# Splitting the queries into high and low parts where they are projected, and loading a layer's small constants earlier

## The chip, the cores and the metric

The kernel runs on one core of one Trainium2 chip. The metric is the device time of one execution in microseconds (us): the median of the runs. The engines are TensorE (PE, with its weight loads PEld), VectorE (DVE), ScalarE (ACT), GpSimd (POOL) and SyncE (SP), which only issues DMAs here. Each takes its own instructions in order.

## What is computed

Two layers of an encoder over a sequence of 2048 positions and 1024 features, in float32. Each layer normalises its input, projects it, sends the parts of the projection through three groups of heads, multiplies each by a gate, and projects back:

```python
for layer in range(2):
    h = rms_norm(x, norm_pre[layer])
    proj = h @ w_in[layer]                      # 1024 -> 4128
    (gq, gk, gv, gg, gaf, gab, dq, dk, dv, dg, hq, hzf, hzb, hi, hg) = split(proj)
    y_a = gla_branch(gq, gk, gv, gg, gaf, gab, wa2_f, ba_f, wa2_b, ba_b, ...)   # gated linear attention
    y_b = diff_branch(dq, dk, dv, dg, lq1, lk1, lq2, lk2, ...)                  # softmax attention
    y_c = hgrn_branch(hq, hzf, hzb, hi, hg, lb, ...)                            # gated recurrence
    x = x + rms_norm(concat(y_a, y_b, y_c) @ w_out[layer], norm_post[layer])
```

The change touches `diff_branch`. It has 4 heads with two softmaxes each, so 8 query and 8 key heads of 64 features. Queries and keys are turned by rotary positions (`x1 cos - x2 sin`, `x2 cos + x1 sin`, on two halves of 32 features), scores are taken, and `w = softmax(s0) - lam * softmax(s1)` weighs the values. `lam` comes from four vectors of 64 numbers per layer. `gla_branch` needs a small matrix of 16 x 128 and a bias of 128 for each direction; these and `lam` are the layer's small constants.

## The kernel before

Matmuls take float32 operands that are split into a rounded high part and the low rest, and add three products (high x high, high x low, low x high). A layer runs in these stages.

**Projection, part 0 and part 1.** The list `first + rest` names 18 blocks of output columns. Part 0 runs all of them for the first 1024 positions, part 1 for the others. A block's weights are loaded by GpSimd's queue in two halves (`wraw`, 512 KB each, one buffer), cast to the high part `whi` on DVE, and the low part `wlo` is made on GpSimd (part 0) or DVE (part 1). Blocks 9 and 10 give the values, 11 and 12 the keys, 13 and 14 the queries (`do_qk`), 15 to 17 the gates (`do_gate`). `do_qk` works on two groups of 512 positions in a part: it loads the rotary table `cs` (512 KB, one buffer), makes two tiles of 512 columns on TensorE (24 matmuls each, line 297), and for each half turns them with two products on DVE (lines 335, 337) and a sum on GpSimd (line 338). A key half is then rounded on ScalarE (line 343), its rest is taken on GpSimd (line 344), and both are stored to `dr_k` in DRAM. A query half is stored once, unsplit, to `dr_q` (line 340). The tiles `u`, `z` and `rh` share one tag of 7 buffers with those of the gates. TensorE writes to 8 banks of PSUM in part 0 and to 4 in part 1. In part 1 the chunked scans of the two other groups of heads are run in between, in steps given by the list `SCHED`; their memory is given back after block 14.

**Attention.** 64 units (4 heads x 16 blocks of 128 queries), in an order written out by hand for TensorE, ScalarE, DVE and GpSimd. For every two units `load_q` fetches 256 queries of both softmaxes: four DMAs of 64 KB, since the rows of each half are wanted twice (the keys' high and low parts lie in 128 partitions), a cast to the high part on GpSimd (line 730) and a subtraction for the low part (line 732). Scores are two matmuls each, `qh` and `ql` against the same keys (lines 875, 876). GpSimd also runs the recurrence of the states (lines 775, 778) at the start of this stage.

**Output projection.** 16 tiles of 128 positions (line 1045); in layer 0 it also opens layer 1's first weights and normalised inputs.

The small constants are loaded in `layer_constants`, after block 0 of part 0: 12 DMAs on SP and some ten short operations, in layer 1 as in layer 0. Block 1 (`do_gate(512, ...)`) yields the low-rank columns `low`, which block 2 transposes (line 414).

The rest of the order is made by a planner ahead of time, from its own estimate of when each operand is ready. SP issues its DMAs in the planned order, and an issue that waits holds up those behind it.

Of the kernel before, what the change touches and what calls it, by code (L numbers as in the profile page):

```python
# [11 lines left out]
F32 = mybir.dt.float32  # L12
F32R = mybir.dt.float32r
BF16 = mybir.dt.bfloat16
U8 = mybir.dt.uint8
AF = mybir.ActivationFunctionType
ALU = mybir.AluOpType
AX = mybir.AxisListType
# [3 lines left out]
P = 128  # L22
L = 2048
# [37 lines left out]
def tile_hybrid_encoder(  # L61
# [9 lines left out]
    nc = tc.nc  # L71

    const = ctx.enter_context(tc.tile_pool(name="const", bufs=1))
    lay = ctx.enter_context(tc.tile_pool(name="lay", bufs=1))
    dram = ctx.enter_context(tc.tile_pool(name="dram", bufs=1, space=DRAM))
# [23 lines left out]
    dr_qh = dram.tile([2, P, L], F32, name="dr_qh")  # L99
    dr_fh = dram.tile([2, 2, P, L], F32, name="dr_fh")  # L100
    dr_kh = dram.tile([2, 2, P, L], F32, name="dr_kh")
    dr_q = dram.tile([8, 2, 32, L], F32, name="dr_q")
    dr_k = dram.tile([8, 2, 2, 32, L], F32, name="dr_k")
    dr_v = dram.tile([L, 512], F32, name="dr_v")
    dr_vs = dram.tile([L, 512], F32, name="dr_vs")
# [17 lines left out]
    def one_bank(shape, name, key="m"):  # L123
        return psum[key][1].tile(shape, F32, tag="one", name=name, bufs=2 if key == "t" else 4)
# [102 lines left out]
    def open_w(l):  # L227
# [9 lines left out]
            nc.gpsimd.tensor_tensor(lo[:, ks], raw, hi[:, ks].bitcast(F32), op=ALU.subtract)  # L237
        return st, (hi, lo)

    for l in range(DEPTH):  # L240
        lam_init = 0.8 - 0.6 * math.exp(-0.3 * l)
        xsrc = x[0] if l == 0 else dr_x
# [1 line left out]

        tst = lay.tile([P, 8, 16], F32, tag="tst", name="tst")
        tots = [lay.tile([P, 2, 16], F32, tag=f"tot_{ti}", name=f"tot_{ti}") for ti in range(3)]
        ls = lay.tile([P, 2], F32, tag="ls", name="ls")
        neglam = lay.tile([P, 1], F32, tag="neglam", name="neglam")
        wa2 = lay.tile([96, 2, P], F32R, tag="wa2", name="wa2")
        ba = lay.tile([P, 2], F32, tag="ba", name="ba")  # L250


        if l == 0:
# [2 lines left out]
        with ExitStack() as s1:  # L256
            ev = s1.enter_context(tc.tile_pool(name=f"ev{l}", bufs=EVB, side="right"))
# [6 lines left out]
            def acc(shape, name, part):  # L264
                turn[0] += 1
                return one_bank(shape, name, "m" if part == 0 and turn[0] % 2 else "s")

            def layer_constants():
                lv = ev.tile([P, 512], F32, tag="t", name="lv").rearrange("p (a n) -> p a n", n=64)
                lp = ev.tile([P, 512], F32, tag="t", name="lp").rearrange("p (a n) -> p a n", n=64)[:, :2]  # L270
                for i, a in enumerate((diff_lq1, diff_lk1, diff_lq2, diff_lk2)):
                    nc.sync.dma_start(lv[:, i], a[l:l + 1].to_broadcast([P, 64]))
                for i in range(2):
                    nc.vector.tensor_tensor(lp[:, i], lv[:, 2 * i], lv[:, 2 * i + 1], op=ALU.mult)
                nc.vector.reduce_sum(ls, lp, axis=AX.X)
                nc.scalar.activation(ls, ls, AF.Exp)
                nc.vector.tensor_tensor(neglam, ls[:, 1:2], ls[:, 0:1], op=ALU.subtract)
                nc.vector.tensor_scalar(neglam, neglam, -lam_init, None, op0=ALU.add)

                wraw = ev.tile([96, 512], F32, tag="t", name="wa").rearrange("p (d n) -> p d n", d=4)[:, :2]  # L280
                nc.vector.memset(wraw, 0.0)
                for d, (wa, b) in enumerate(((gla_wa2_fwd, gla_ba_fwd), (gla_wa2_bwd, gla_ba_bwd))):
                    for i in range(3):
                        nc.sync.dma_start(wraw[32 * i + 16 * d:32 * i + 16 * d + 16, d], wa[l])
                    nc.sync.dma_start(ba[:, d:d + 1], b[l].unsqueeze(1))
                nc.vector.tensor_copy(wa2, wraw)
                nc.vector.tensor_tensor(wa2[64:96], wraw[64:96], wa2[64:96].bitcast(F32), op=ALU.subtract)

            def wload(c0, n, part, halves=False):
                return wload_into(wp, l, nc.gpsimd if part == 0 else nc.vector, c0, n, halves)  # L290
# [33 lines left out]
            def do_qk(c0, cb, which, part):  # L324
                hc = slice(4 * cb, 4 * cb + 4)
                w = wload(c0 + 256 * cb, 256, part, halves=True)
                for g in (2 * part, 2 * part + 1):
                    sl = slice(g * 512, (g + 1) * 512)
                    cs = ev.tile([P, 2, 512], F32, tag="cs", name="cs", bufs=1)
                    nc.sync.dma_start(cs, c_rope[0 if which == "q" else 1, :, :, sl])  # L330
                    p1 = mm_ch(w, 0, g)
                    p2 = mm_ch(w, P, g)
                    for half, (a, b, op) in enumerate(((p1, p2, ALU.subtract), (p2, p1, ALU.add))):
                        u = ev.tile([P, 512], F32, tag="t", name="ru")
                        nc.vector.tensor_tensor(u, a, cs[:, 0], op=ALU.mult)  # L335
                        z = ev.tile([P, 512], F32, tag="t", name="rz")
                        nc.vector.tensor_tensor(z, b, cs[:, 1], op=ALU.mult)
                        nc.gpsimd.tensor_tensor(u, u, z, op=op)
                        if which == "q":
                            nc.sync.dma_start(dr_q[hc, half, :, sl], u)  # L340
                        else:
                            rh = ev.tile([P, 512], F32R, tag="t", name="rh")
                            nc.scalar.copy(rh, u)
                            nc.gpsimd.tensor_tensor(u, u, rh.bitcast(F32), op=ALU.subtract)
                            nc.sync.dma_start(dr_k[hc, half, 0, :, sl], rh.bitcast(F32))
                            nc.sync.dma_start(dr_k[hc, half, 1, :, sl], u)

# [132 lines left out]
            for i, b in enumerate(first + rest):  # L480
                b(0)
                if i == 0:
                    w_st.close()
                    xp_st.close()
                    hp = w_in_st.enter_context(tc.tile_pool(name=f"hp{l}", bufs=1, side="right"))
                    hhi += [hp.tile([P, 4, KC, P], F32R, name=f"hhi{g}") for g in (2, 3)]
                    hlo += [hp.tile([P, 4, KC, P], F32R, name=f"hlo{g}") for g in (2, 3)]
                    if l == 0:
                        load_constants()
                    layer_constants()  # L490
                if N0 < i <= N0 + 8:
                    prenorm_split(xn, (i - N0 - 1) % 4, hhi[2 + (i - N0 - 1) // 4], hlo[2 + (i - N0 - 1) // 4])
                if N0 <= i < N0 + 8:
                    xn = prenorm_load(npre, 8 + i - N0, ev, xsrc)
# [226 lines left out]
                kv[h] = (ks, v)  # L721

            def load_q(h, qp):
                qr = ak.tile([P, 2, 256], F32, tag="aq", name="aq", bufs=2)
                for half in range(2):
                    for s in range(2):
                        p0 = 64 * half + 32 * s
                        nc.sync.dma_start(qr[p0:p0 + 32], dr_q[2 * h:2 * h + 2, half, :, qp * 256:(qp + 1) * 256].rearrange("c p t -> p c t"))
                qh = ak.tile([P, 2, 256], F32R, tag="aqh", name="aqh", bufs=2)
                nc.gpsimd.tensor_copy(qh, qr)  # L730
                ql = ak.tile([P, 2, 256], F32R, tag="aql", name="aql", bufs=2)
                nc.gpsimd.tensor_tensor(ql, qr, qh.bitcast(F32), op=ALU.subtract)  # L732
                ga = ak.tile([P, 2, P], F32, tag="aga", name="aga", bufs=3)
                nc.sync.dma_start(
                    ga, dr_gate[qp * 256:(qp + 1) * 256, 256 + h * P:384 + h * P].rearrange("(j p) n -> p j n", p=P))
                qs_of[h, qp] = qh, ql, ga

            emitted = [0]
            for i, b in enumerate(first + rest):
                b(1)  # L740
                scans(LAG * SCHED[i] if i < SC_END else len(work))
                if i == SC_END:
# [4 lines left out]
                    ak = at_st.enter_context(tc.tile_pool(name=f"ak{l}", bufs=1, side="left"))  # L747
# [7 lines left out]
        with ExitStack() as s2:  # L755
# [14 lines left out]
            for i in range(14):  # L770
                for d in range(2):
                    c, sh = (i + 1, 1) if d == 0 else (14 - i, -1)
# [188 lines left out]
            with tc.manual_schedule(engines={getattr(mybir.EngineType, e) for e in ENGINES}):  # L961
                for f in range(4 * NU + 13):
# [51 lines left out]
                    if fw == 4 * KC + 8:  # L1014
                        wr_st.close()
                        op = s2.enter_context(tc.tile_pool(name=f"op{l}", bufs=2, side="right"))
# [51 lines left out]
            if l + 1 < DEPTH:  # L1068
                h_st, hhi, hlo, npre = open_h(l + 1)
                nc.sync.dma_start(npre, norm_pre[l + 1:l + 2].to_broadcast([P, D]))  # L1070
                w_st, w_first = open_w(l + 1)
                ep = s2.enter_context(tc.tile_pool(name=f"ep{l}", bufs=EPB, side="left"))
            for t in range(NT):
                y1, y2 = y2, out_prep(t + 1) if t + 1 < NT else None
                o = out_tile(t, *y1)
                if l + 1 < DEPTH:
                    if 1 <= t <= 8:
                        g, i = divmod(t - 1, 4)
                        prenorm_split(xn, i, hhi[g], hlo[g])
                    if t < 8:  # L1080
                        xn = next_scale(o)
# [53 lines left out]
```

## Time and profile before

| | |
|---|---|
| median of 3 runs | 3637.28 us (3628.71 to 3641.9) |
| profiled execution | 3641.44 us, span 3639.6 us |
| mean granted TensorE clock | 0.982 |
| TensorE busy | 3513.4 us (97%) |
| DVE, ScalarE, GpSimd busy | 2560.3, 1927.8, 1459.6 us (70%, 53%, 40%) |
| DMA | 430.49 MB, 118 GB/s over the span |

The span goes from the first to the last instruction; the execution's own time is 1.8 us longer. A matmul's end is modelled, so a busy TensorE need not be at its peak.

### The profile page before, as it was taken

The page shows a single profiled execution, that of the slowest core. Times are in us where ns is not written, and L with a number is a line of the kernel's source. Part 1 is how long each engine was busy: PE and PEld are TensorE (multiplying, and loading weights), DVE is VectorE, ACT ScalarE, POOL GpSimd, SP SyncE. Part 2 cuts the span into 40 slices and gives each one's busy share as a digit, 9 for nine tenths or more (in the row PEclk, how much of TensorE's full clock was granted, in tenths as well). Part 3 has the DMA queues.
Part 4 walks back from the last instruction along what each step waited for, and adds up shares of the span by engine and source line. Part 5 has one row for each costly group of instructions (what it writes and reads, how often), then busy time and mean ns, then how long its engine had stood idle before and what let it go on. Part 6 is the DMA issues. An engine that isn't in the chain of part 4 may idle for free.

```text
span 3639.6 us, 62254 instructions
## 1 busy us (share of the span) xinstructions
PE 3513.4 (97%) x23296; PEld 3159.5 (87%) x23296; DVE 2560.3 (70%) x4426; ACT 1927.8 (53%) x4340; POOL 1459.6 (40%) x1454
## 2 busy tenths in 40 slices
PE   8999999998989999999989999999999899999999
PEld 7898988987978999888878989889878799999887
DVE  5422699987389999985324227999863899999733
ACT  4520455542377888874225215555423778888722
POOL 4545410012476667720035454100125867767100
PEclk9999999998999999999999999999989999999999
DMA  4444544544441333213334444445444413322143
GB/s 155 127 139 134 151 128 139 157 126 139 136 133 34 120 109 97 73 43 132 120 109 128 140 136 139 140 145 154 133 123 141 125 42 120 118 83 73 34 139 116
DMA packets 293645, 430.49 MB, mean 118 GB/s; under 512 B 42400, under 2 KB 185312, under 8 KB 291040
## 3 DMA queue, kind: packets, MB, share of 16 engines
q1 hardware_dynamic: 268896, 333.71, 29.7%
q0 software_dynamic: 22336, 90.71, 8.4%
q8 instruction: 184, 3.01, 0.3%
q10 hardware_dynamic: 2112, 2.10, 0.2%
q14 instruction: 117, 0.96, 0.1%
HBM read 275.82 MB, written 152.57 MB: 118 GB/s over the span
## 4 chain that ended last, share of the span: by engine, by line
PE 67%; DVE 13%; DMA 10%; POOL 4%; issue 3%; ACT 1%; SPq 1%; DVEq 0%; POOLq 0%; ACTq 0%
PE pp L306 14%; PE pp L297 12%; PE pob L1045 10%; PE po L938 9%; PE s L875 5%; PE s L876 5%; PE pt L927 5%; DMA wraw<-in_w_in_dram 3%; DVE mx L880 3%; DMA cs<-c_rope 2%; PE pm L587 2%; DVE e L921 2%; PE pm L568 1%; DMA ust<-dr_u 1%; PE poi L825 1%
## 5 line engine op out<-in xcount | busy, mean ns | idle before, releaser
L880 DVE TENSOR_REDUCE mx<-s 128x1 f32<-128x1024 f32 x512 | 623.1, 1217 | 54.3 <-PE s L876 52.9
L889 ACT ACTIVATE e<-s,mx 128x1024 f32<-128x1024 f32 x512 | 571.7, 1121 | 74.8 <-DVE mx L880 53.3
L306 PE MATMUL pp<-wlo,hhi 128*128 128x256 f32 (+1 forms) x2048 | 589.1, 288 | 7.1 <-POOL wlo L224 6.8
L306 PE MATMUL pp<-whi,hhi 128*128 128x256 f32 (+1 forms) x2048 | 585.2, 286 | 5.5 <-DVE ru L335 4.5
L306 PE MATMUL pp<-whi,hlo 128*128 128x256 f32 (+1 forms) x2048 | 588.4, 287 | 0.5 <-DVE hlo L195 0.5
L938 PEld LDWEIGHTS po<-vt,wt 128*128 128x128 f32 x4096 | 537.6, 192 | 47.9 <-ACT o L945 5.8
L938 PE MATMUL po<-vt,wt 128*128 128x128 f32 x4096 | 544.0, 276 | 1.6 <-ACT o L945 1.6
L875 PE MATMUL s<-ks,aqh 128*128 128x512 f32 x1024 | 452.4, 442 | 19.8 <-ACT e L889 15.1
L214 POOL DMA_DIRECT2D wraw<-in_w_in_dram x124 | 96.0, 774 | 920.4 <-DVE wlo L224 348.6
L876 PE MATMUL s<-ks,aql 128*128 128x512 f32 x1024 | 407.2, 398 | 14.2 <-POOL aql L732 14.1
L297 PE MATMUL pp<-hhi,whi 128*128 128x512 f32 x1024 | 412.5, 403 | 0.0
L297 PE MATMUL pp<-hlo,whi 128*128 128x512 f32 x1024 | 411.2, 402 | 0.0
L297 PE MATMUL pp<-hhi,wlo 128*128 128x512 f32 x1024 | 409.0, 399 | 0.0
L306 PEld LDWEIGHTS pp<-wlo,hhi 128*128 128x128 f32 x2048 | 390.0, 190 | 10.5 <-POOL wlo L224 7.6
L306 PEld LDWEIGHTS pp<-whi,hhi 128*128 128x128 f32 x2048 | 391.9, 191 | 8.0 <-issue 4.8
L921 DVE SCALAR_TENSOR_TENSOR e<-e,gam 128x1024 f32<-128x1024 f32 x256 | 392.3, 1533 | 0.0
L306 PEld LDWEIGHTS pp<-whi,hlo 128*128 128x128 f32 x2048 | 390.5, 191 | 1.8 <-DVE hlo L195 0.7
L931 ACT COPY wt<-pt 128x512 f32<-128x512 f32 x512 | 301.3, 589 | 118.9 <-PE pt L927 115.7
L927 PE MATMUL pt<-ident,e 128*128 128x128 f32 x2048 | 310.1, 274 | 1.2 <-ACT wt L931 0.6
L927 PEld LDWEIGHTS pt<-ident,e 128*128 128x128 f32 x2048 | 241.9, 142 | 2.9 <-ACT wt L931 1.2
L875 PEld LDWEIGHTS s<-ks,aqh 128*128 128x128 f32 x1024 | 196.4, 192 | 51.7 <-ACT e L889 23.3
L297 PEld LDWEIGHTS pp<-hhi,whi 128*128 128x128 f32 x1024 | 194.6, 190 | 45.0 <-issue 0.9
(190 smaller groups left out, 7042.9 us busy)
## 6 DMA issues: line engine op xcount, KB each, us to landing
wraw<-in_w_in_dram POOLq DMA_DIRECT2D x116, 512.0 KB, 4.8
cs<-c_rope SPq DMA_DIRECT2D x32, 512.0 KB
dr_gate<-z SPq DMA_DIRECT2D x64, 256.0 KB
aq<-dr_q SPq DMA_DIRECT2D x256, 64.0 KB
ks<-dr_k POOLq DMA_DIRECT2D x16, 1024.0 KB, 8.0
y<-dr_y SPq DMA_DIRECT2D x32, 512.0 KB
dr_qs<-qt SPq DMA_DIRECT2D x48, 256.0 KB
qs<-dr_qs SPq DMA_DIRECT2D x24, 512.0 KB
```

What stands on the lines that cost most here:

```text
L214: nc.gpsimd.dma_start(raw[:, :, :n], w_in[l].rearrange("(k p) c -> p k c", p=P)[:, ks, c0:c0 + n])
L297: nc.tensor.matmul(ps.rearrange("p (a t) -> p a t", t=P), w[a][:, k, c:c + P], b[g][:, :, k], start=n == 0, stop=n == 3 * KC - 1)
L306: nc.tensor.matmul(ps, b[g][:, t % 4, k], w[a][:, k, :n], start=cnt == 0, stop=cnt == 3 * KC - 1)
L875: nc.tensor.matmul(s[:, i], self.qh[:, c, js], kk, start=True, stop=False)
L876: nc.tensor.matmul(s[:, i], self.ql[:, c, js], kk, start=False, stop=True)
L880: nc.vector.tensor_reduce(mx[:, k:k + 1], self.s[k].rearrange("p a n -> p (a n)"), axis=AX.X, op=ALU.max, negate=True)
L889: nc.scalar.activation(self.es[c][:, n * 1024:(n + 1) * 1024], self.s[kk].rearrange("p a n -> p (a n)"), AF.Exp, bias=self.mx[:, m:m + 1], ...
L921: nc.vector.scalar_tensor_tensor(es[0][:, hs], es[1][:, hs], gm[:, 8 + n:9 + n], es[0][:, hs], op0=ALU.mult, op1=ALU.add)
L927: nc.tensor.transpose(pt[:, i], self.es[0][:, (4 * q + i) * P:(4 * q + i + 1) * P], ident)
L931: nc.scalar.copy(wt, self.pt[q])
L938: nc.tensor.matmul(self.po, self.wt[q][:, i], self.v[:, k], start=k == 0, stop=k == NT - 1)
L1045: nc.tensor.matmul(pos[:, n], a[:, k], b[k][:, n * 512:(n + 1) * 512], start=cnt == 0, stop=cnt == 3 * KC - 1)
```

## The change

Queries are split as keys are: a half is rounded on ScalarE, its rest taken on GpSimd, and both parts are stored, each twice, to a `dr_q` that is laid out as the attention wants it. `load_q` becomes two plain loads of 256 KB, with no work on GpSimd. `layer_constants` and the tiles that it fills are moved out of the layer's stage; layer 0 calls it where it did, and for layer 1 it is called in layer 0's output projection, with the tiles of that stage's pool `ep`.

```diff
-    dr_q = dram.tile([8, 2, 32, L], F32, name="dr_q")
+    dr_q = dram.tile([8, 2, 2, 2, 32, L], F32, name="dr_q")
...
+    def layer_tiles():
+        neglam = lay.tile([P, 1], F32, tag="neglam", name="neglam")
+        wa2 = lay.tile([96, 2, P], F32R, tag="wa2", name="wa2")
+        ba = lay.tile([P, 2], F32, tag="ba", name="ba")
+        return neglam, wa2, ba
+
+    def layer_constants(l, pool, neglam, wa2, ba):
+        ls = lay.tile([P, 2], F32, tag="ls", name="ls")
...
+        if l == 0:
+            neglam, wa2, ba = consts = layer_tiles()
+        else:
+            neglam, wa2, ba = consts
...
+                        rh = ev.tile([P, 512], F32R, tag="t", name="rh")
+                        nc.scalar.copy(rh, u)
+                        nc.gpsimd.tensor_tensor(u, u, rh.bitcast(F32), op=ALU.subtract)
                         if which == "q":
-                            nc.sync.dma_start(dr_q[hc, half, :, sl], u)
+                            for dup in range(2):
+                                nc.sync.dma_start(dr_q[hc, 0, half, dup, :, sl], rh.bitcast(F32))
+                                nc.sync.dma_start(dr_q[hc, 1, half, dup, :, sl], u)
                         else:
-                            rh = ev.tile([P, 512], F32R, tag="t", name="rh")
-                            nc.scalar.copy(rh, u)
-                            nc.gpsimd.tensor_tensor(u, u, rh.bitcast(F32), op=ALU.subtract)
                             nc.sync.dma_start(dr_k[hc, half, 0, :, sl], rh.bitcast(F32))
                             nc.sync.dma_start(dr_k[hc, half, 1, :, sl], u)
...
                     if l == 0:
                         load_constants()
-                    layer_constants()
+                        layer_constants(0, ev, *consts)
...
             def load_q(h, qp):
-                qr = ak.tile([P, 2, 256], F32, tag="aq", name="aq", bufs=2)
-                for half in range(2):
-                    for s in range(2):
-                        p0 = 64 * half + 32 * s
-                        nc.sync.dma_start(qr[p0:p0 + 32], dr_q[2 * h:2 * h + 2, half, :, qp * 256:(qp + 1) * 256].rearrange("c p t -> p c t"))
                 qh = ak.tile([P, 2, 256], F32R, tag="aqh", name="aqh", bufs=2)
-                nc.gpsimd.tensor_copy(qh, qr)
                 ql = ak.tile([P, 2, 256], F32R, tag="aql", name="aql", bufs=2)
-                nc.gpsimd.tensor_tensor(ql, qr, qh.bitcast(F32), op=ALU.subtract)
+                for i, q in enumerate((qh, ql)):
+                    nc.sync.dma_start(q.bitcast(F32), dr_q[2 * h:2 * h + 2, i, :, :, :, qp * 256:(qp + 1) * 256]
+                                      .rearrange("c a d p t -> (a d p) c t"))
...
                 ep = s2.enter_context(tc.tile_pool(name=f"ep{l}", bufs=EPB, side="left"))
+                consts = layer_tiles()
+                layer_constants(l + 1, ep, *consts)
```

## Rows read from the trace of the kernel before

**Rows 1.** The page's first line.

```profile
span 3639.6 us, 62254 instructions
```

**Rows 2.** Waits of PE: line <- releaser: us in total, times, longest us.

```profile
PE s L876 <- POOL aql L732: 14.1, 4, 4.3
...
PE ppa L414 <- ACT low L390: 11.4, 3, 5.1
...
PE s L875 <- POOL aqh L730: 3.6, 2, 3.0
```

**Rows 3.** Timeline of DVE, start of layer 1: start, us, work [idle before <- releaser].

```profile
1871.35 0.23 DVE L274 TENSOR_TENSOR lp<-lv 128x64 f32<-128x64 f32 x1 [12.52 <-DMA lv<-in_diff_lk_dram]
...
1879.18 0.29 DVE L286 CAST wa<-wa 96x256 fp32r<-96x256 f32 x1 [4.11 <-DMA wa<-in_gla_wa_bwd_dram]
```

**Rows 4.** Chain (start, us, what) and a stretch of the windows, both layers' start.

```profile
76.75 4.85 PE pp L297 x21
...
1889.38 7.45 PE pp L297 x21
core 0: us, PE busy (x) PEld busy (x) DVE busy (x) ACT busy (x) POOL busy (x), PEclk, DMA share, GB/s
1889.00:1897.00 8.00, 8.00 (x24) 6.28 (x25) 3.53 (x4) 3.77 (x8) 7.53 (x6) 0.63 0.29 86
```

**Rows 5.** Groups by line, GpSimd: busy us, mean ns of one, idle before.

```profile
L732 POOL TENSOR_TENSOR aql<-aq,aqh 128x512 fp32r<-128x512 f32 x64 | 88.1, 1376 | 4.9
...
L344 POOL TENSOR_TENSOR ru<-ru,rh 128x512 f32<-128x512 f32 x32 | 42.3, 1322 | 21.4 <-ACT rh L343 18.6 <-DMA cs<-c_rope 2.0 <-DMA tst<-tot 0.7
...
L730 POOL CAST aqh<-aq 128x512 fp32r<-128x512 f32 x64 | 40.3, 630 | 35.1 <-DMA aq<-dr_q 25.2 <-PE s L875 9.9
```

**Rows 6.** Windows: four stretches of the attention, and layer 0's whole attention.

```profile
1050.00:1070.00 20.00, 15.10 (x87) 13.41 (x88) 13.84 (x24) 11.19 (x25) 19.17 (x17) 0.83 0.30 91
1090.00:1110.00 20.00, 16.90 (x98) 14.99 (x97) 14.31 (x27) 11.80 (x29) 19.21 (x17) 0.83 0.10 27
2860.00:2880.00 20.00, 13.97 (x83) 12.37 (x82) 11.56 (x21) 10.22 (x24) 19.13 (x18) 0.83 0.42 141
2910.00:2920.00 10.00, 7.13 (x32) 6.47 (x32) 4.49 (x5) 2.72 (x9) 9.52 (x10) 0.66 0.17 48
...
1001.00:1631.00 630.00, 612.98 (x4285) 559.79 (x4286) 588.09 (x1024) 512.85 (x1202) 409.93 (x480) 0.98 0.29 86
```

**Rows 7.** DMA issues: queue, count, KB each.

```profile
cs<-c_rope SPq DMA_DIRECT2D x32, 512.0 KB
...
dr_q<-ru SPq DMA_DIRECT2D x32, 256.0 KB
```

**Rows 8.** Windows: a stretch of layer 0's query blocks, part 0.

```profile
312.50:320.50 8.00, 8.00 (x37) 6.47 (x36) 3.09 (x5) 0.00 (x0) 2.66 (x2) 1.00 0.26 102
```

**Rows 9.** Timeline of DVE, layer 0, part 0: first rotary product of each group.

```profile
278.76 0.69 DVE L335 TENSOR_TENSOR ru<-pp,cs 128x512 f32<-128x512 f32 x1 [4.26 <-DMA cs<-c_rope]
...
291.66 0.69 DVE L335 TENSOR_TENSOR ru<-pp,cs 128x512 f32<-128x512 f32 x1 [9.73 <-DMA cs<-c_rope]
...
306.22 0.69 DVE L335 TENSOR_TENSOR ru<-pp,cs 128x512 f32<-128x512 f32 x1 [4.17 <-DMA cs<-c_rope]
...
316.42 0.69 DVE L335 TENSOR_TENSOR ru<-pp,cs 128x512 f32<-128x512 f32 x1 [7.71 <-DMA cs<-c_rope]
...
324.13 0.69 DVE L335 TENSOR_TENSOR ru<-pp,cs 128x512 f32<-128x512 f32 x1 [4.63 <-DMA cs<-c_rope]
...
338.73 0.69 DVE L335 TENSOR_TENSOR ru<-pp,cs 128x512 f32<-128x512 f32 x1 [4.20 <-DMA cs<-c_rope]
```

**Rows 10.** Chain (start, us, what) and one row of SP's timeline, layer 0.

```profile
361.81 45.79 PE pp L306 x370
...
917.39 3.58 DMA dr_u<-ut
...
923.11 13.86 DMA cs<-c_rope
...
884.21 1.70 SPq L340 DMA_DIRECT2D dr_q<-ru  x2
```

More of the change, by code (lines that the diff above doesn't have):

```diff
@@ L238, in open_w @@
         return st, (hi, lo)
+    def layer_tiles():
[5 more added lines that the diff above has]
+        ls = lay.tile([P, 2], F32, tag="ls", name="ls")
+        lam_init = 0.8 - 0.6 * math.exp(-0.3 * l)
+        lv = pool.tile([P, 512], F32, tag="t", name="lv").rearrange("p (a n) -> p a n", n=64)
+        lp = pool.tile([P, 512], F32, tag="t", name="lp").rearrange("p (a n) -> p a n", n=64)[:, :2]
+        for i, a in enumerate((diff_lq1, diff_lk1, diff_lq2, diff_lk2)):
+            nc.sync.dma_start(lv[:, i], a[l:l + 1].to_broadcast([P, 64]))
+        for i in range(2):
+            nc.vector.tensor_tensor(lp[:, i], lv[:, 2 * i], lv[:, 2 * i + 1], op=ALU.mult)
+        nc.vector.reduce_sum(ls, lp, axis=AX.X)
+        nc.scalar.activation(ls, ls, AF.Exp)
+        nc.vector.tensor_tensor(neglam, ls[:, 1:2], ls[:, 0:1], op=ALU.subtract)
+        nc.vector.tensor_scalar(neglam, neglam, -lam_init, None, op0=ALU.add)
+        wraw = pool.tile([96, 512], F32, tag="t", name="wa").rearrange("p (d n) -> p d n", d=4)[:, :2]
+        nc.vector.memset(wraw, 0.0)
+        for d, (wa, b) in enumerate(((gla_wa2_fwd, gla_ba_fwd), (gla_wa2_bwd, gla_ba_bwd))):
+            for i in range(3):
+                nc.sync.dma_start(wraw[32 * i + 16 * d:32 * i + 16 * d + 16, d], wa[l])
+            nc.sync.dma_start(ba[:, d:d + 1], b[l].unsqueeze(1))
+        nc.vector.tensor_copy(wa2, wraw)
+        nc.vector.tensor_tensor(wa2[64:96], wraw[64:96], wa2[64:96].bitcast(F32), op=ALU.subtract)
     for l in range(DEPTH):
@@ L246, in tile_hybrid_encoder @@
         tots = [lay.tile([P, 2, 16], F32, tag=f"tot_{ti}", name=f"tot_{ti}") for ti in range(3)]
[L247 to L250, printed above, removed]
+        if l == 0:
+            neglam, wa2, ba = consts = layer_tiles()
+        else:
+            neglam, wa2, ba = consts
         if l == 0:
@@ L266, in acc @@
                 return one_bank(shape, name, "m" if part == 0 and turn[0] % 2 else "s")
[L268 to L287, printed above, removed]
             def wload(c0, n, part, halves=False):
```

## The prediction

> **What bounds the kernel now.** I read the page, then the table of waits by engine, then the timeline and the chain in the places where TensorE waits, and last the DMA share in short stretches. The span is 3639.6 us [rows 1] and TensorE is busy for 97% of it, so every sum below is made in TensorE's time: how much idle or half-clock time a step takes out or puts in. Its three waits that this change can touch are small: 11.4 us before the transposes of the low-rank gate, 14.1 and 3.6 us in the attention for the low and high parts of the queries [rows 2]. In the rotary stage of the projection a second bound runs close beside TensorE, the queue of DMAs that SP issues, and that is where I expect this change to be decided.
>
> **Layer 1's constants.** In layer 1 the vector engine stood 12.52 us at the first product of the lambda vectors, whose loads SP had issued behind the stores of the first projection, and 4.11 us at the small decay weight [rows 3]. The copies of the gate tiles queue behind these on DVE, ScalarE's copies of the low-rank columns behind those, and TensorE waits 11.4 us [rows 2]. Its clock then falls: from 1889 to 1897 the granted clock is 0.63, a mix of the 2.4 and the 1.2 GHz level, and the first 21 matmuls of the next block take 7.45 us. The same 21 matmuls of layer 0, where the constants came early, take 4.85 us [rows 4]. Moved to layer 0's output projection, the loads have that whole stage as cover. Gain: 11.4 + 2.6 = 14.0 us, less about 1 us for the last gate tile's own copies: **13 us** (bounds 8 and 14; what is late next is the do_gate copies, at TensorE's own pace). Price at the new place: 12 DMA issues on SP and eight short DVE operations (0.23 and 0.29 us [rows 3]), beside 16 tiles of 48 matmuls on TensorE, each 11.1 us by the 4.85 us for 21. Since a tile's operands are made one tile ahead, I take nothing; if DVE stood at the loads there as long as at the second of these waits, and nothing hid it, it would be 4 us.
>
> **The attention's split.** Removed are 64 casts of 630 ns and 64 subtractions of 1376 ns on GpSimd, 40.3 + 88.1 = 128 us [rows 5]. Almost all lies beside TensorE. It counts only where GpSimd is full with the state scan: in the four stretches of [rows 6], 70 us in all, GpSimd is busy for 67, TensorE for 53, at granted clocks of 0.66 to 0.83. The two waits make 17.7 us [rows 2]; the half clock behind each costs some 2 us more, five times. But DVE is the next limit: over layer 0's whole attention it is busy for 588 of 630 us, and in the four stretches it stands idle for 70 - 44.2 = 25.8 us [rows 6], so no more than 25 us can come back. I take **20 us** (bounds 0, if ScalarE's exponentials become the wait, and 25).
>
> The new loads, two of 256 KB for each pair of query blocks in place of four of 64 KB, have the time of two pairs to land, and the DMA share over the attention is 0.29 [rows 6]: nothing. GpSimd also waited for the first queries of each layer, 25.2 us in two waits [rows 5], but what stood behind them (the last rotary sums) had its own inputs only then: nothing, at most 2 us each.
>
> **The split where queries are projected.** Each half gets a ScalarE cast and a GpSimd subtraction of 1322 ns, as the keys have [rows 5]; 32 of each. The keys bear them in the same place beside a TensorE that is busy for 8.00 of 8.00 us where this stage was looked at [rows 8]. Nothing for these; without that cover a half would cost up to 2 us. What counts is the stores. Each half stored one tile of 256 KB; now it stores four (high and low part, each twice). That is 32 stores becoming 128 [rows 7].
>
> How long does one take? From 312.5 to 320.5 us only stores of this shape are left in flight, and the share of the 16 DMA engines stands at 0.26 with 102 GB/s [rows 8]: as if four engines worked and twelve were idle. One store is then 262144 B / 102 GB/s = 2.57 us (an estimate), one after another. A load on all engines (the rotary table cs, a weight half wraw, 512 KB each) puts 1/16 on each, 32 KB at 25.5 GB/s = 1.29 us. The key blocks store four tiles per group of 512 positions: 4 x 2.57 + 2 x 1.29 = 12.9 us; the rows give 291.66 - 278.76 = 12.9 us between groups. Query blocks store two: 2 x 2.57 + 2 x 1.29 = 7.7 us; the rows give 324.13 - 316.42 = 7.7 us [rows 9]. So the pace of the groups is already that of four DMA engines wherever it isn't TensorE's 48 matmuls (11.1 us by the 21 in 4.85 us [rows 4]), because cs has one buffer and its load queues behind the stores. With eight stores a group takes 8 x 2.57 + 2.58 = **23.1 us**, twice TensorE's.
>
> The Trainium skill (DMA: Bandwidth & Descriptors, "Why a DMA increments its semaphore by 16 and not by 1") says that a DMA runs on the largest number of engines, up to 16, that divides the slowest dimension of both its patterns; the destination here has 4 heads outermost, before and after, which would be four. By the same page's fit for the transfer part (bytes / 436e3 us) a store would be an estimated 0.6 us, eight would fit under TensorE's 11 us, and the kernel would be faster by what the other two parts give. The share of 0.26 speaks for the first of the two rules.
>
> First pass (part 0): the keys' queue is as before, so the first query group is worked on at 306.2 and the second at 316.4; then 339.5 and 362.6, the last one before was at 338.73 [rows 9]. The casts of the gate's weights stand between these on DVE, and 23 us after the last group TensorE could start the next gate block, at 361.81 [rows 10]. The same steps after 362.6 give 385.7: **+24 us** a layer. Bounds: 0, since the eight PSUM banks let TensorE run four groups ahead and weights cast earlier would fill the gap; and 34, since the seven buffers of the shared tag are held by waiting stores, four more of 2.57 us.
>
> Second pass (part 1): the first query stores go out at 884.21 [rows 10]. The last cs lands behind 24 stores: 884.2 + 24 x 2.57 = 945.9, plus 1.3 for its own share or the 13.86 us that it took beside the first K and V loads: 947 to 960, where it came at 923.11 + 13.86 = 937.0 [rows 10]. TensorE waits for that group's banks: +10 to +23, **+16 us** a layer. The release of the scan's memory by the dr_u store (3.58 us [rows 10]) queues there as well, and so the K load. Bounds 0 and 30.
>
> Sum: 3641.4 us (the profiled execution) - 13 - 20 + 2 x (24 + 16) = 3688.4. The median of the runs lies 4.2 us below that execution, so **3684 us**, 1.3% slower.
>
> **Rivals.**
> *Stores hidden.* The place is DVE's order in the rotary stage: if the gates' weight casts come ahead of the delayed groups, TensorE has 23 us of gate matmuls (338.73 to 361.81 [rows 9, 10]) to lay over a delay of 24, and its banks to put them in. I price what is left at a third of the 24 + 16, 13 us a layer with the clock. Time 3637 - 33 + 26 = 3630. It decides at a loss of 33 us over the four passes, what the other two parts give: below that the kernel isn't slower. Against it: the last cast that the gates waited for in part 0 stood behind the rotary products, 23 us after the last group [rows 9, 10], and DVE takes its work in order.
> *Sixteen engines.* If the new layout spreads the stores, each costs half of what a load of 512 KB costs an engine, 0.65 us; at any price under (11.1 - 2.6) / 8 = 1.06 us the queue keeps up, and 3637 - 33 = 3604 remains. Against it: the plateau of [rows 8].
> *The queue reaches the attention.* The last stores of part 1 hold SP's ring until 980 or so; gate stores, state and output weights come after them, buffers stay taken, and another 15 to 20 us a layer goes: about 3720.
>
> **Chances.** Forecast (3655 to 3705) 0.58; stores hidden 0.17; sixteen engines 0.06; queue reaching the attention 0.19. Half a per cent, 18 us, is about what a measurement of this kernel can tell. Slower: nearly all of the first, and the last, 0.76. Same: most of hidden and an edge of the first, 0.15. Faster: sixteen engines and an edge of hidden, 0.09. Range 3628 to 3738: it takes in half of the hidden case and the attention case with its upper bound.
>
> **What would show it.** Query groups on DVE 23 us apart in part 0 of both layers, a DMA share near 0.26 through the stage, idle TensorE of some 20 us with a lower granted clock before the gate blocks; a wait for cs of 20 us or more near 950; no wait of TensorE before the low-rank transposes of layer 1; no wait for aql in the attention. The prediction is wrong if groups stay at 11 us, if TensorE stays busy at the gates though they don't, or if the attention doesn't shorten.

## The result and the profile after

The changed kernel takes 3750.0 us in the median (3747.5 to 3754.6, four runs), the kernel before 3635.6 in the same place: a ratio of 1.0316, 95% interval 1.0294 to 1.0339, 3.2% slower. The profiled execution:

```profile
span 3749.8 us, 62098 instructions
```

To see where the 110 us between the two spans lie, I cut both traces at the first matmul of each stage (us; part 0 runs from the first channel block to the first transposed key of the scan, part 1 from there to the first scores, then the attention, then the output projection up to the next layer's first channel block):

| stage | before | after | difference |
|---|---|---|---|
| layer 0, part 0 | 400.2 | 437.3 | +37.1 |
| layer 0, part 1 | 520.6 | 553.6 | +33.0 |
| layer 0, attention | 633.4 | 622.8 | -10.6 |
| hand-over to layer 1 | 258.3 | 248.6 | -9.7 |
| layer 1, part 0 | 401.0 | 438.3 | +37.3 |
| layer 1, part 1 | 520.9 | 552.9 | +32.0 |
| layer 1, attention | 630.6 | 621.2 | -9.4 |

First the two parts that gain. Waits of TensorE in the changed kernel, as in [rows 2]:

```profile
PE pp L314 <- DVE whi L223: 50.6, 13, 10.3
PE pp L314 <- DVE ru L343: 48.7, 2, 24.5
PE pp L314 <- POOL wlo L224: 23.0, 10, 4.3
...
PE s L881 <- DMA aqh<-dr_q: 10.6, 2, 5.5
...
PE ppa L424 <- ACT low L400: 2.1, 2, 1.7
```

The wait for the low-rank columns fell from 11.4 to 2.1 us, and no wait for the queries' low part is left. Behind the low-rank columns, the 21 matmuls of [rows 4] take 4.87 us, where they took 7.45; the granted clock from 1938 to 1946 is 1.00 (the chain, start of layer 1):

```profile
1939.57 4.87 PE pp L305 x21
```

That is 2.6 us less for these, inside layer 1's part 0; with the 9.7 of the hand-over the constants give 12.3 us. The new waits, 50.6 + 48.7 + 23.0 us for weights and rotary products, are all in the projections. DVE's timeline in layer 0, part 0, the query groups and what follows, beside [rows 9]:

```profile
306.44 0.69 DVE L343 TENSOR_TENSOR ru<-pp,cs 128x512 f32<-128x512 f32 x1 [4.33 <-DMA cs<-c_rope]
...
321.80 0.69 DVE L343 TENSOR_TENSOR ru<-pp,cs 128x512 f32<-128x512 f32 x1 [12.23 <-DMA cs<-c_rope]
...
346.13 0.69 DVE L343 TENSOR_TENSOR ru<-pp,cs 128x512 f32<-128x512 f32 x1 [11.92 <-DMA cs<-c_rope]
...
368.56 0.69 DVE L343 TENSOR_TENSOR ru<-pp,cs 128x512 f32<-128x512 f32 x1 [15.92 <-DMA cs<-c_rope]
...
385.18 0.69 DVE L403 COPY z<-pp 128x512 f32<-128x512 f32 x1 [4.57 <-DMA dr_q<-ru]
...
391.60 0.69 DVE L403 COPY z<-pp 128x512 f32<-128x512 f32 x1 [2.85 <-DMA dr_q<-rh]
...
398.05 0.69 DVE L329 SCALAR_TENSOR_TENSOR lsm<-z,lse 128x512 f32<-128x512 f32 x1 [5.76 <-DMA dr_q<-ru]
...
403.12 0.69 DVE L403 COPY z<-pp 128x512 f32<-128x512 f32 x1 [4.38 <-DMA dr_q<-rh]
```

The last two groups begin 24.3 and 22.4 us after the one before. Behind the last, DVE doesn't wait for the rotary table any more but for tiles: the gates' copies (lines 403 and 329) need buffers of the shared tag, and by the waits shown these are free only when a query store has landed. The windows of the same place:

```profile
316.00:328.00 12.00, 12.00 (x54) 9.73 (x53) 3.18 (x5) 0.62 (x1) 4.44 (x4) 1.00 0.26 102
...
359.00:388.00 29.00, 9.61 (x43) 8.52 (x42) 4.56 (x7) 3.22 (x5) 11.08 (x9) 0.59 0.46 157
388.00:408.00 20.00, 19.11 (x159) 18.70 (x157) 4.07 (x6) 5.87 (x9) 6.33 (x5) 1.00 0.33 122
408.00:420.00 12.00, 3.30 (x12) 2.71 (x12) 4.74 (x6) 6.42 (x10) 9.82 (x7) 0.66 0.28 84
```

The DMA share stands at 0.26 with 102 GB/s, as in [rows 8], but for twelve microseconds on end. TensorE is busy for 9.61 of 29 us and then for 3.30 of 12, at granted clocks of 0.59 and 0.66. The chain between names the stores (the time of a DMA row is that from its issue to its landing), and behind them the gates' copies and the next gate block's weights:

```profile
360.33 2.44 SPq L353
...
362.87 2.33 SPq L352
...
370.29 14.77 DMA dr_q<-ru
...
389.49 13.51 DMA dr_q<-rh
...
403.12 0.70 DVE z L403
...
409.81 2.31 POOL wlo L224
...
412.41 4.35 DMA wraw<-in_w_in_dram
...
416.78 0.71 DVE whi L223
...
420.35 4.85 PE pp L314 x21
```

Part 1 looks alike; its last query group waits 28.66 us for its table:

```profile
998.25 0.69 DVE L343 TENSOR_TENSOR ru<-pp,cs 128x512 f32<-128x512 f32 x1 [28.66 <-DMA cs<-c_rope]
```

### The profile page after: what moved, and what is told of

Same layout as the page of the kernel before. It is cut to its first block, busy times and chain, and to the rows that moved or that the text cites. A ratio compares the mean times of both kernels' runs of the same rounds, so it can differ in the third digit from the quotient of the medians.

```text
span 3749.8 us, 62098 instructions
## 1 busy us (share of the span) xinstructions
PE 3523.0 (94%) x23296; PEld 3172.6 (85%) x23296; DVE 2514.4 (67%) x4426; ACT 1944.4 (52%) x4372; POOL 1374.5 (37%) x1358
## 4 chain that ended last, share of the span: by engine, by line
PE 64%; DMA 15%; DVE 8%; POOL 5%; issue 4%; SPq 3%; ACT 2%; DVEq 0%; POOLq 0%; ACTq 0%
PE pp L314 11%; PE po L944 11%; PE pp L305 10%; PE pob L1051 9%; PE s L881 5%; PE s L882 5%; PE pt L933 5%; DMA wraw<-in_w_in_dram 3%; DMA dr_q<-rh 3%; DMA cs<-c_rope 2%; DMA dr_q<-ru 2%; PE pm L578 1%; PE pm L597 1%; DMA dr_u<-ut 1%; DMA qs<-dr_qs 1%
## 5 line engine op out<-in xcount | busy, mean ns | idle before, releaser
L314 PE MATMUL pp<-whi,hhi 128*128 128x256 f32 (+1 forms) x2048 | 595.8, 291 | 99.7 <-DVE whi L223 50.6
L314 PE MATMUL pp<-wlo,hhi 128*128 128x256 f32 (+1 forms) x2048 | 599.0, 293 | 27.4 <-POOL wlo L224 23.0
L314 PE MATMUL pp<-whi,hlo 128*128 128x256 f32 (+1 forms) x2048 | 596.6, 291 | 0.3 <-DVE hlo L195 0.3
L314 PEld LDWEIGHTS pp<-whi,hhi 128*128 128x128 f32 x2048 | 401.1, 196 | 104.7 <-DVE whi L223 53.6
L881 PE MATMUL s<-ks,aqh 128*128 128x512 f32 x1024 | 451.8, 441 | 23.5 <-ACT e L895 12.1
L314 PEld LDWEIGHTS pp<-wlo,hhi 128*128 128x128 f32 x2048 | 398.9, 195 | 33.1 <-POOL wlo L224 25.6
L314 PEld LDWEIGHTS pp<-whi,hlo 128*128 128x128 f32 x2048 | 399.9, 195 | 1.5 <-DVE hlo L195 0.5
L927 DVE SCALAR_TENSOR_TENSOR e<-e,gam 128x1024 f32<-128x1024 f32 x256 | 346.5, 1354 | 0.0
L348 ACT CAST rh<-ru 128x512 fp32r<-128x512 f32 x64 | 39.6, 619 | 385.8 <-POOL ru L346 329.8
L881 PEld LDWEIGHTS s<-ks,aqh 128*128 128x128 f32 x1024 | 196.0, 191 | 50.6 <-ACT e L895 15.2
```

Of the source, the lines that this page charges most:

```text
L314: nc.tensor.matmul(ps, b[g][:, t % 4, k], w[a][:, k, :n], start=cnt == 0, stop=cnt == 3 * KC - 1)
L881: nc.tensor.matmul(s[:, i], self.qh[:, c, js], kk, start=True, stop=False)
L927: nc.vector.scalar_tensor_tensor(es[0][:, hs], es[1][:, hs], gm[:, 8 + n:9 + n], es[0][:, hs], op0=ALU.mult, op1=ALU.add)
```

## The experiments

Theory: a store of a rotated tile runs on four DMA engines, 2.57 us for 256 KB; 32 of them in a pass hold the queue, and the tiles that wait in it hold back the gates. Rivals: the added casts and subtractions, the number of issues on SP, the order in SP's queue. All ratios are to the kernel before, on the same chip, with 95% intervals. Two runs that are compared in us can be from different chips, on which the kernel before took 3635.6 to 3640.6 us in the median; where that matters, the difference by the ratios is given too. Stages and waits are those of one profiled execution. Code is cut where `...` stands.

| run | median us | ratio | interval |
|---|---|---|---|
| constants_alone | 3627.4 | 0.9968 | 0.9956 to 0.9981 |
| stores_alone | 3783.8 | 1.0401 | 1.0379 to 1.0423 |
| q_wide | 3608.4 | 0.9910 | 0.9892 to 0.9928 |
| q_once | 3634.5 | 0.9988 | 0.9975 to 1.0001 |
| q_eight | 3646.4 | 1.0018 | 1.0004 to 1.0032 |
| evb6 | 3772.4 | 1.0367 | 1.0344 to 1.0389 |
| q_wide_evb6 | 3617.4 | 0.9935 | 0.9917 to 0.9953 |
| cs_pool | 3776.7 | 1.0376 | 1.0352 to 1.0401 |
| all_wide | 3565.5 | 0.9797 | 0.9776 to 0.9818 |
| wide_no_split | 3592.7 | 0.9868 | 0.9851 to 0.9885 |

**constants_alone.** The move of the constants, with the query split undone.

> The kernel before with nothing changed but layer 1's constants, loaded in layer 0's output projection. By the step of the prediction: 13 us less, 3636 - 13 = 3623; by the two traces, in which the stretch from the output projection to the 21st matmul of the next block went from 266.15 to 253.74 us, 12.4 less: 3623 again. Rival: the wait that is gone there comes back later in layer 1, as a queue that was already behind, and the time stays at 3636.

Measured 10.7 us less, by the interval 7 to 16. The hand-over takes 248.8 us as in the changed kernel. The step holds, and nothing is given back.

**stores_alone.** The kernel before with three more stores of each query tile.

```
 nc.sync.dma_start(dr_q[hc, half, :, sl], u)
+for i in range(3):
+    nc.sync.dma_start(dr_qx[hc, i, half, :, sl], u)
...
```

> The kernel before with each rotated query tile stored four times, the three added stores into memory that nothing reads; no split, no cast, the attention and the constants as before. Theory (stores on four engines, 23.1 us for a group, and tiles held by them after the last group): the whole loss and no gain, 3636 + 142 = 3778; a tile is held by four stores in place of two tiles by two each, so the held buffers should come to the same: 3760 to 3790. The prediction's sizes of 24 and 16 us a pass would give 3636 + 80 = 3716. Rival (the split's operations are the cost): 3636 to 3650.

Measured +145.7 us. Parts 0 grow by 43.7 and 42.6 us, parts 1 by 28.1 and 29.4; the attention stays at 632. So the stores by themselves make the whole loss: 145.7, less 10.7 for the constants and 20.0 for the attention (10.6 + 9.4), is 115, and the change cost 114.4. They lose somewhat more in parts 0 and less in parts 1 than the change does.

**q_wide.** The same stores at another place in DRAM.

```
-dr_q = dram.tile([8, 2, 2, 2, 32, L], F32, name="dr_q")
+dr_q = dram.tile([2, 2, 2, 2, P, L], F32, name="dr_q")
-nc.sync.dma_start(dr_q[hc, 0, half, dup, :, sl], rh.bitcast(F32))
+nc.sync.dma_start(dr_q[cb, 0, half, dup, :, sl], rh.bitcast(F32))
...
```

> The changed kernel with another layout of the queries' copy in DRAM: the four heads of a tile lie one behind the other, so that a store writes 128 rows at one stride; as many stores of as many bytes, each tile as long held by its two stores. The loads in the attention become four of 32 partitions in place of one of 128. Theory (four engines for each store are the cost): on sixteen engines a store takes 0.64 us, a group 8 x 0.64 + 2.58 = 7.7 us, under TensorE's 11.1, and only the gains are left, 3636 - 12 - 20 = 3604, between 3596 and 3615. Rival one (the cast, the subtraction and one more buffer for each half cost the time): 3720 to 3750. Rival two (the number of stores that SP must issue, 2 to 3 us each, costs it): 3700 to 3750.

Measured 3608.4: the loss is gone and the gains are left, with every cast, subtraction, buffer and issue of the change still there. Both rivals that price these fall. The window in which only query stores are in flight, and the first products of query groups two to four:

```profile
314.00:318.00 4.00, 4.00 (x19) 3.26 (x18) 0.50 (x1) 0.00 (x0) 0.34 (x1) 1.00 1.02 392
```

```profile
317.50 0.69 DVE L343 TENSOR_TENSOR ru<-pp,cs 128x512 f32<-128x512 f32 x1 [8.40 <-DMA dr_q<-ru]
...
330.90 0.69 DVE L343 TENSOR_TENSOR ru<-pp,cs 128x512 f32<-128x512 f32 x1 [1.94 <-DMA cs<-c_rope]
...
343.04 0.69 DVE L343 TENSOR_TENSOR ru<-pp,cs 128x512 f32<-128x512 f32 x1 [8.95 <-DMA cs<-c_rope]
```

The share is 1.02 in place of 0.26 and the rate 392 GB/s in place of 102, so 262144 / 392e3 = 0.67 us a store. The groups are 13.4 and 12.1 us apart, near TensorE's 11.1, not 23.

**q_once.** High and low part stored once and loaded twice, still on four engines.

> The changed kernel with the high and the low part stored once, not twice: four stores for a group of 512 positions in place of eight, still on four engines; the attention loads each copy twice, in loads of 32 partitions. Theory (the time of the stores on four engines): 4 x 2.57 + 2.58 = 12.9 us for a group, the keys' pace, 1.8 us over TensorE's 11.1, so that a pass is late by some 7 us at its end, of which banks and weights take a part: 3604 + 4 x (0 to 7) = 3604 to 3632. Rival (casts, subtractions and the added buffer): they are all still there, 3720 to 3750.

Measured 3634.5, 26 us above q_wide and 2 above my range. Parts 0 take 406.1 and 412.6 us (q_wide 398.6 and 402.0), parts 1 527.4 and 526.9 (516.3 and 520.4): 7.5, 10.6, 11.1 and 6.5 us a pass, 36 in all. But this profiled execution lies 9 us above the run's median, so by the medians a pass costs 6 to 7 us on average, the upper end of the 0 to 7 that I had allowed. A group that is only 1.8 us slower than TensorE's still costs that much.

**q_eight.** q_wide with a gap of one row after every 16.

```
-dr_q = dram.tile([2, 2, 2, 2, P, L], F32, name="dr_q")
+dr_q = dram.tile([2, 2, 2, 2, 8, 17, L], F32, name="dr_q")
-nc.sync.dma_start(dr_q[cb, 0, half, dup, :, sl], rh.bitcast(F32))
+nc.sync.dma_start(dr_q[cb, 0, half, dup, :, :16, sl], rh.bitcast(F32))
...
```

> The kernel q_wide with a gap of one row behind every 16 rows in DRAM, so that a store writes 8 pieces of 16 rows; the loads in the attention take 16 partitions each. Eight stores a group as in the changed kernel. Theory (a store runs on as many engines, up to 16, as divide its slowest dimension): eight engines, 1.29 us a store, 8 x 1.29 + 2.58 = 12.9 us a group, as with four stores on four engines (q_once, 26 us above q_wide): 3608 + 26 = 3634, between 3622 and 3645. Rival one (any pattern in pieces is slow alike): as the changed kernel, 3750. Rival two (the pieces don't matter, something else in q_wide's layout does): as q_wide, 3608.

```profile
347.00:354.00 7.00, 7.00 (x61) 7.00 (x61) 3.18 (x5) 0.62 (x1) 4.57 (x4) 1.00 0.53 203
```

Half the engines and half the rate: 1.29 us a store. Its query groups begin at 319.34, 334.64 and 347.97, as q_once's at 318.84, 333.70 and 347.38: twice the stores at half the price. The four passes cost 24 us over q_wide, as expected (26); the time is 12 us above the forecast, and 1 above its range, because the attention takes 629.1 and 630.4 us, 6 and 8 more than in q_wide. There TensorE waits 27.1 us for loaded queries, 15.0 in q_wide; that the loads of 16 partitions are the reason is likely and was not tested. By the Trainium skill (DMA: Bandwidth & Descriptors, "Why a DMA increments its semaphore by 16 and not by 1") the destination's slowest dimension of 4, 8 or 128 gives 4, 8 or 16 engines; the three shares of 0.26, 0.53 and 1.02 agree.

**evb6 and q_wide_evb6.** One buffer fewer (`EVB = 6`), in the changed kernel and in q_wide.

> The changed kernel with six buffers of the shared tag in place of seven, nothing else. Theory (what the prediction sized too small is the tiles held by the waiting stores: after the last query group the gates' tiles wait for them): a tile is held by two stores of 2.57 us, so one buffer fewer lets every later step of a pass begin 5.1 us later, four passes, 3750 + 20 = 3770, between 3760 and 3785. Rival (the loads and stores that stand behind the query stores in SP's queue set the end, whatever buffers there are): 3745 to 3755.

> The control for evb6: q_wide with six buffers of the shared tag in place of seven. Theory (a buffer matters because the waiting stores hold it): with stores of 0.64 us a tile is held 1.3 us, not 5.1, so four passes cost at most 5 us: 3608 to 3613. Rival (this kernel needs seven buffers in its other steps, whatever the stores): 20 us or more, 3628 and above.

Measured +22 us (18 by the ratios) and +9 us. Waits of DVE for landed stores, changed kernel with six buffers (lines of dr_q alone; with seven buffers such lines add up to 99.8 us):

```profile
DVE lsm L329 <- DMA dr_q<-rh: 81.7, 8, 12.1
DVE rz L345 <- DMA dr_q<-rh: 55.4, 10, 7.7
DVE ru L343 <- DMA dr_q<-ru: 31.4, 8, 5.1
...
DVE z L403 <- DMA dr_q<-ru: 8.7, 2, 4.4
...
DVE rz L345 <- DMA dr_q<-ru: 7.6, 2, 3.9
...
DVE lsm L329 <- DMA dr_q<-ru: 7.1, 2, 3.6
```

These are 191.9 us in place of 99.8. Much of that is the same idle time under another name: DVE's wait for the rotary tables falls from 223.3 to 192.2 us, and that for the gates' weights (line 223) from 125.5 to 64.0. What shows that the tiles are short is the time itself, inside the range of the theory. But the control came out between its two cases. More than half of its waits of DVE for stores of queries and keys (26.5 of 48.8 us) are for the keys', which are on four engines there too:

```profile
DVE ru L343 <- DMA dr_k<-ru: 14.1, 8, 4.0
DVE rz L345 <- DMA dr_k<-rh: 10.1, 4, 3.1
```

So some 13 of evb6's 22 us (9 of 18 by the ratios) belong to the query stores, 9 to steps that both kernels share. The theory had put all 20 down to the query stores; that its total came out is partly luck.

**cs_pool.** The rotary tables through GpSimd's queue.

```
-nc.sync.dma_start(cs, c_rope[0 if which == "q" else 1, :, :, sl])
+nc.gpsimd.dma_start(cs, c_rope[0 if which == "q" else 1, :, :, sl])
```

> The changed kernel with the rotary tables loaded through GpSimd's queue in place of SP's, so that they no longer stand behind the query stores. Theory (the four engines' time and the seven buffers set the pace): the next group's products then wait for tiles instead; four groups still need 4 x 8 x 2.57 = 82 us of stores in a pass beside TensorE's 44, only the tables' own share of 1.29 us and the gap behind them fall out, 4 to 10 us a pass: 3710 to 3735. Rival (the order in SP's queue is the cost): TensorE's 48.7 us of waits for the rotary products and a good part of the 74 us for the gates' weights go, 3650 to 3690.

A miss for both: 27 us slower than the changed kernel (22 by the ratios). The last three keys' groups and the first query group follow one another by 14.8 to 17.6 us, each waiting for its table, so that the query groups begin at 316.08 (306.44). Then tiles are late inside the groups, and the tables still between some:

```profile
348.56 0.69 DVE L343 TENSOR_TENSOR ru<-pp,cs 128x512 f32<-128x512 f32 x1 [6.16 <-DMA dr_q<-ru]
355.23 0.69 DVE L343 TENSOR_TENSOR ru<-pp,cs 128x512 f32<-128x512 f32 x1 [5.38 <-DMA dr_q<-rh]
...
369.03 0.69 DVE L343 TENSOR_TENSOR ru<-pp,cs 128x512 f32<-128x512 f32 x1 [7.51 <-DMA cs<-c_rope]
...
376.90 0.69 DVE L343 TENSOR_TENSOR ru<-pp,cs 128x512 f32<-128x512 f32 x1 [4.45 <-DMA dr_q<-rh]
...
394.80 0.69 DVE L403 COPY z<-pp 128x512 f32<-128x512 f32 x1 [10.25 <-DMA dr_q<-ru]
```

DVE waits for tiles inside the groups, and the first gate copy waits 10.25 us for a store. But the tables are late on GpSimd's queue too (DVE waits 159.3 us for them, 223.3 in the changed kernel), so this run alone does not clear the order in SP's queue. q_wide says more: there the tables stand behind as many stores in the same queue, and the loss is gone. How the 27 us divide between the keys' late tables and the rest I did not separate.

**all_wide.** q_wide with the keys' copy laid out alike and the queries stored once.

```
-dr_k = dram.tile([8, 2, 2, 32, L], F32, name="dr_k")
+dr_k = dram.tile([2, 2, 2, P, L], F32, name="dr_k")
-nc.gpsimd.dma_start(k, dr_k[2 * h + c].rearrange("a s p t -> (a s p) t"))
+for a in range(4):
+    r = 64 * (h % 2) + 32 * c
+    nc.gpsimd.dma_start(k[32 * a:32 * a + 32], dr_k[h // 2, a // 2, a % 2, r:r + 32])
...
```

> The kernel q_wide with the keys' copy laid out in the same way (stores of 128 rows at one stride) and the queries stored once, not twice; the keys' loads become four of 32 partitions. Theory: a key group needs 4 x 0.64 + 2.58 = 5.1 us of the queue in place of 12.9, under TensorE's 11.1; what TensorE still waits for in the rotary stage of q_wide is 5.7 us for the products and 4.2 us for the gates' weights, so at most 10 us come back: 3598 to 3608. Rival (four times as many loads of the keys, issued by GpSimd, delay the start of the attention): 3610 to 3630.

3565.5 us, 2.0% faster than the kernel before and 43 us below q_wide, where I expected 10 at most. Parts 0 take 392.0 and 392.1 us, parts 1 505.5 and 508.6: 39 of the 43 us are in the projections. TensorE's waits there (9.9 us for products and weights in q_wide) are gone, but the larger part is in other places, such as the wait of 18.3 us before the scan's transposes (9.2 here: 4.4 for products, 3.6 of issue, 1.2 for ScalarE) and the clock: over 400 to 480 us the granted clock is 0.94 in q_wide and 1.00 here:

```profile
400.00:480.00 80.00, 75.26 (x610) 73.24 (x609) 74.46 (x132) 42.90 (x103) 17.67 (x15) 1.00 0.52 150
```

How much of the 43 us is the keys' stores and how much the halved query stores wasn't separated.

**wide_no_split.** all_wide with the queries split in the attention, as before.

> all_wide without the query split: the constants moved, keys and queries stored as 128 rows at one stride, the queries unsplit, cast and subtracted in the attention as before. It prices the split once the stores are cheap. By the two traces the attention is 10.6 and 9.4 us shorter with the split: 3565 + 20 = 3585, between 3577 and 3592. Rival (once the stores no longer hold the queue, GpSimd's casts in the attention are hidden): 3560 to 3570.

27 us above all_wide (26 by the ratios), just above my range. The attention takes 633.7 and 633.0 us in place of 620.2 and 620.4, and the two waits of [rows 2] are back:

```profile
PE s L885 <- POOL aqh L740: 15.7, 2, 8.4
PE s L886 <- POOL aql L742: 6.2, 2, 3.1
```

So the split itself is worth 26 us where its stores are cheap.

## Why the prediction went wrong

**Right: layer 1's constants.** 13 us forecast, 12.3 by the stages, 10.7 by the run of that part alone (interval 7 to 16).

**Right: the attention.** 20 us forecast, 20.0 by the stages (10.6 + 9.4). The rival in which the queue reaches the attention does not hold for its length; only its first queries come late (10.6 us), and they do so in q_wide and all_wide too (12.9 us in both), whose query stores are short.

**Right: four engines, 2.57 us a store, 23.1 us a group.** The groups are 24.3 and 22.4 us apart, and the runs with 16 and 8 engines take the loss away in the measure of the engines. Casts, subtractions and issues cost nothing that shows: q_wide has them all.

**Wrong in size: what the stores cost TensorE.** Forecast 24 and 16 us a layer, 80 in all. Measured 37 + 33 in layer 0, and 40 + 32 in layer 1 (37.3 and the 2.6 that the constants gave back there), 142 in all. The step that failed is that one delay is priced for each pass, and nothing for the gate blocks behind it. The projection's matmuls run in the same order in both traces, so TensorE's lateness can be read at one and the same matmul, by counting. It grows in two places in each pass (us):

| where it grows | forecast | layer 0 | layer 1 |
|---|---|---|---|
| part 0, weights of the second gate block | 24 | 21 | 23 |
| part 0, weights of the third gate block | 0 | 15 | 15 |
| part 1, banks of the last query group | 16 | 22 | 22 |
| part 1, gate blocks behind it | 0 | 10 | 13 |

Matmuls of TensorE in layer 0 where the first three rows begin or end, kernel before:

```profile
361.81 0.39 PE L306 MATMUL pp<-wlo,hhi 128*128 128x256 f32 x1 [1.93 <-POOL wlo L224]
...
386.25 0.28 PE L306 MATMUL pp<-wlo,hhi 128*128 128x256 f32 x1
...
939.92 0.36 PE L306 MATMUL pp<-whi,hhi 128*128 128x256 f32 x1 [2.17 <-DVE ru L335]
```

The same three matmuls in the changed kernel:

```profile
383.09 0.58 PE L314 MATMUL pp<-wlo,hhi 128*128 128x256 f32 x1 [1.63 <-POOL wlo L224]
...
420.35 0.58 PE L314 MATMUL pp<-wlo,hhi 128*128 128x256 f32 x1 [2.02 <-POOL wlo L224]
...
1000.28 0.55 PE L314 MATMUL pp<-whi,hhi 128*128 128x256 f32 x1 [24.54 <-DVE ru L343]
```

- **Part 0, the forecast delay.** The step "the same steps after 362.6 give 385.7" came out, at 383.09, but partly by luck. The last group began at 368.56 and not at 362.6, since the second group's table stood behind two stores of the first (321.80 in place of 316.4). And the block followed it by 14.5 us, not by the 23 of before. In the kernel before, its second cast had stood for its weights' load, and not only behind the rotary products as the prediction has it:

```profile
358.63 0.69 DVE L223 CAST whi<-wraw 128x1024 fp32r<-128x1024 f32 x1 [8.72 <-DMA wraw<-in_w_in_dram]
```

- **Part 0, behind it.** In the kernel before the third gate block runs without a wait. In the changed kernel its casts, at 406.66 and 416.78 on DVE, come behind the gates' copies, four of which wait 2.85 to 5.76 us each for tiles that stores of the last two groups still hold (eight stores a group, 20.6 us). The chain above goes from such a store over the copy at 403.12 to the weights' low part at 409.81, a load of 4.35 us, and the matmul at 420.35. There TensorE is 34.1 us late, 21.3 at 383.09; the rest of the 15 comes behind it, while the granted clock is 0.73 (420 to 430 us).
- **Part 1, the forecast delay.** The last group begins 61.2 us later than before, of which 37.6 are the late start of the pass (514.3 in place of 476.7). The rest, 23.6, is the upper end of my 10 to 23, not the 16 that I took.
- **Part 1, behind it.** The first gate copy and the operation on it (line 329) wait 3.81 and 9.62 us for query stores, and a cast of the next block's weights comes behind them, at 1017.13.

The forecast lacks 30 us in layer 0. The two places taken at nothing make 25, the longer wait in part 1 makes 6, and the first delay came out 3 us shorter; some 2 us lie in other places. I had named this hold as the upper bound in part 0 (34 us, tiles "held by waiting stores") and then taken the figure without it; in part 1 it stands nowhere. All four passes came out 2 to 6 us above their upper bounds. It isn't shown that the terms behind the last groups are of tiles alone, since loads of weights stand in the same chain and SP's gate stores queue in the same place; evb6 puts a price on one tile, 9 to 13 us over the four passes.

The rival in which the stores are hidden needed a loss below 33 us over four passes; it was 142.

## What to carry to other kernels

Before a tile of 128 partitions is stored to a scratch tensor, look at the first dimension of the DRAM pattern: a layout for the reader (4 heads outermost) can leave the store a quarter of the engines, and a plain 128-row stride with the loads cut up instead gave 142 us back here, and another 43 once the keys had it too and the queries were stored once. Price added stores as a stream: count of stores times the time of one from the DMA share, from the first issue to the last landing, and let the next stage begin when the tiles come free, not when the last group's arithmetic is done. A queue that is near its limit costs more than the waits that name it.

## What I had not expected

- The kernel before already paid for its four-engine stores of keys and queries, although TensorE is busy for 8.00 of 8.00 us beside them [rows 8]: wide_no_split does the work of constants_alone with sixteen engines for these and is 35 us faster (3592.7 and 3627.4), the parts 0 by 5.7 and 7.8 us, the parts 1 by 11.4 and 5.6.
- When the queue is full, SP's issues themselves take nearly as long as a store: 2.44 and 2.33 us each in the chain above, 0.51 us for a key store at 297.49.
- Twice the engines gave twice the rate with little loss: 102, 203 and 392 GB/s on four, eight and sixteen.
